# Softmax attention in a tuned encoder block: queries' preparation written behind the scores, and a bias made by two operations in place of three

## The chip, the cores and the metric

The kernel runs on one core of a Trainium2 chip. A core has five engines that work side by side and wait for each other by semaphores: TensorE (PE, matrix products and transposes), VectorE (DVE), ScalarE (ACT), GpSimd (POOL) and SyncE (SP, which here only issues transfers). Each engine works through its own instructions strictly in order. PE writes its results into PSUM, from which DVE and ACT read them. The metric is device time in microseconds (us), as a median over runs.

## The reference, cut to what matters

One encoder layer on x of 1024 tokens by 1024 features, in float32: gated linear attention (GLA) beside windowed attention (SWA), both projected, gated and merged, then a SwiGLU feed-forward part. The change lies in SWA alone: 8 query heads, 2 key/value heads, head width 128, tokens in 8 blocks of 128, each block of queries looking at up to three blocks of keys.

```python
q = _rope(_rms_norm(q, q_g), pos); k = _rope(_rms_norm(k, k_g), pos)
scores = jnp.einsum("bnqhgd,bnkhd->bnhgqk", qb, kc) * (hd ** -0.5)
scores = jnp.where(mask, scores, -jnp.inf)
m = jnp.maximum(scores.max(axis=-1, keepdims=True), sink)
p = jnp.exp(scores - m)
denom = p.sum(axis=-1, keepdims=True) + jnp.exp(sink - m)
o = jnp.einsum("bnhgqk,bnkhd->bnqhgd", p / denom, vc)
```

## The kernel before

**Products.** Each float32 operand of a large product is split into a high part (ACT, a copy that rounds) and a low part (DVE, the difference), and a product is made of three matmuls: high by high, high by low, low by high. So each weight tile costs ACT one operation (`wh`, L70) and DVE one (`wl`, L72).

**The attention stage** works on 16 items: 2 groups of four query heads (g) by 8 blocks of queries (n). An item goes through these steps, one per slot of the loop:

- `a_load` fetches the raw queries `qr` by a transfer that SP issues.
- `a_prep`: the mean of squares (ACT `sq` L866, DVE `ss` L867), its inverse root `rs` (ACT `rl` L98 and L99, DVE L101 to L104), and the rotary positions (DVE L912, L914, L916, L917, which write `qn`). PE does nothing here.
- `a_turn`: PE turns the four heads over (L923), ACT takes the high part `sqh` from PSUM (L926), DVE the low part `sql` (L927). `k_turn` does the same for a block of keys (PE L900, ACT `kTh` L902, DVE `kTl` L903), and `k_prep` splits the values (ACT `vSh` L894, DVE `vSl` L895), in the first half alone.
- `a_scores`, once per head: three matmuls (L76, names `kTh,sqh`, `kTl,sqh`, `kTh,sql`), then DVE adds the band's mask, writes `p` and takes the row maximum `mx` (L941). After the fourth head DVE works out the bias `nm` (L948 to L950) and `es` (L952), ACT makes the four exponentials with bias `nm` and scale `rs` (L956, with row sums `dn`), DVE the inverse of the sum (`dn` L958, `rd` L960), POOL multiplies (`p` L962). The normalised scale of the queries, `rs`, is thus applied to the scores, not to the queries.
- `a_probs`, once per block of keys: PE turns `p` over (L973), ACT and DVE split it (`ph` L976, `pl` L977).
- `a_out`: up to nine matmuls (L76, names `ph,vSh`, `pl,vSh`, `ph,vSl`), ACT copies the result out (`sob` L987), SP stores it.

In a slot, different steps of different items stand behind each other. A tuple `order` sets in which order the steps of one slot are written down. Behind each step, `slot` spends its share of a number n of dense matmuls (L76, names `mm`, from projections that have nothing to do with attention): 26 per slot in the first two slots, then 15, so about one behind each of 14 steps. A step that gives PE nothing to do still takes its share.

**What sets the order on an engine.** On PE, the order of writing holds exactly (`manual_schedule`). On DVE, ACT, POOL and SP a scheduler orders instructions when the program is built; the order of writing is its priority, its own estimate of when an operand is ready decides the rest. The order is then fixed, and each engine waits at its next instruction.

**PSUM buffers.** All attention products and transposes take turns in four buffers (`ch`), the dense ones in four others (`mm`). A `ch` buffer comes free when ACT or DVE has read it last: `pl` for a transposed block of p, L941 for a head's scores, `sql` and `kTl` for turned queries and keys, `sob` for the output. Which buffer a new product gets is fixed at build time too.

Of the kernel before, what the change touches and what calls it, by code (L numbers as in the profile page):

```python
# [12 lines left out]
ALU = mybir.AluOpType  # L13
# [17 lines left out]
def body(tc, i, out):  # L31
    nc = tc.nc
    with ExitStack() as root:
# [8 lines left out]
        def nm(s):  # L42
            uid[0] += 1
            return f"{s}_{uid[0]}"
# [4 lines left out]
        def chtile(shape, dt=F32):  # L49
            return psc.tile(list(shape), dt, tag="ch", name=nm("ch"))  # L50
# [27 lines left out]
        def mm3(o, ah, al, bh, bl, start, stop):  # L78
            mm(o, ah, bh, start, False)
            mm(o, ah, bl, False, False)  # L80
            mm(o, al, bh, False, stop)
# [798 lines left out]
        def k_load(t):  # L880
            raws[t] = sw.tile([P, 256], F32, tag="kvr", name=nm("kvr"))
            need(("skv", t))
            nc.sync.dma_start(out=raws[t], in_=scr["skv", t][:, 256:512])
            keys[t] = sw.tile([P, 2, P], F32, tag="key", name=nm("key"))
            nc.sync.dma_start(out=keys[t].rearrange("p a b -> p (a b)"), in_=scr["key", t])
# [45 lines left out]
        def a_scores(g, n, h):  # L931
            a = att[g, n]
            if h == 0:
                a.p = sw.tile([P, 4, 384], F32, tag="p", name=nm("p"))
                a.mx = sw.tile([P, 4], F32, tag="mx", name=nm("mx"))
            w, p, mx = a.w, a.p, a.mx
            ks = slice(a.b0 * P, (a.b1 + 1) * P)
            mo = (a.b0 - (n - 1)) * P
            s = chtile((P, 384))
            mm3(s[:, :w], a.qh[:, h], a.ql[:, h], kTh[:, g, ks], kTl[:, g, ks], True, True)  # L940
            nc.vector.tensor_tensor_reduce(out=p[:, h, :w], in0=s[:, :w], in1=band[:, mo:mo + w],  # L941
                                           op0=ALU.add, op1=ALU.max, scale=1.0, scalar=-1e30,
                                           accum_out=mx[:, h:h + 1])
            if h < 3:
                return
            sk = sink[:, 4 * g:4 * g + 4]
            nm_ = sw.tile([P, 4], F32, tag="nm", name=nm("nm"))
            nc.vector.tensor_tensor(mx, mx, a.rs, op=ALU.mult)  # L948
            nc.vector.tensor_tensor(mx, mx, sk, op=ALU.max)
            nc.vector.tensor_scalar(nm_, mx, -1.0, None, op0=ALU.mult)  # L950
            es = sw.tile([P, 4], F32, tag="es", name=nm("es"))
            nc.vector.tensor_tensor(es, sk, mx, op=ALU.subtract)  # L952
            nc.scalar.activation(es, es, AF.Exp)
            dn = sw.tile([P, 4], F32, tag="dn", name=nm("dn"))
            for h in range(4):
                nc.scalar.activation(p[:, h, :w], p[:, h, :w], AF.Exp, bias=nm_[:, h:h + 1],  # L956
                                     scale=a.rs[:, h:h + 1], accum_out=dn[:, h:h + 1])
            nc.vector.tensor_tensor(dn, dn, es, op=ALU.add)  # L958
            rd = sw.tile([P, 4], F32, tag="rd", name=nm("rd"))
            nc.vector.reciprocal(rd, dn)  # L960
            for h in range(4):
                nc.gpsimd.tensor_scalar(p[:, h, :w], p[:, h, :w], rd[:, h:h + 1], None, op0=ALU.mult)  # L962
# [50 lines left out]
        for n in range(2 * KT):  # L1013
            g, t = divmod(n, KT)
            todo[n + 5].append((a_out, g, t))
            todo[n + 5] += [(a_probs, g, t, kb) for kb in range(3)]
            todo[n + 3] += [(a_scores, g, t, h) for h in range(4)]
            todo[n + 2].append((a_turn, g, t))
            todo[n + 1].append((a_prep, g, t))
            if n < KT:  # L1020
                todo[n + 1].append((k_turn, n))
                todo[n].append((k_prep, n))
                if n:
                    todo[n - 1].append((k_load, n))
            todo[n].append((a_load, g, t))
        order = (a_probs, k_prep, a_prep, a_scores, a_turn, k_turn, a_out, k_load, a_load)
        k_load(0)
        with tc.manual_schedule(engines={mybir.EngineType.PE}):
            for t, v in enumerate(todo):
# [507 lines left out]
```

## Time and profile before

| What | us |
|---|---|
| Median of 3 runs | 1645.83 (1645.22 to 1646.64) |
| The profiled execution's own time | 1645.61 |
| Its span (first to last instruction) | 1643.8 |
| PE busy | 1626.0 (99%) |
| DVE busy | 1251.4 (76%) |
| ACT busy | 842.6 (51%) |
| POOL busy | 76.0 (5%) |

The profile is of one execution. Busy time is the time in which an engine had an instruction running. A wait stands at the instruction that had to wait, with what released it. In a row of the timeline the first number is the start in us from the span's start, the second the duration. DVE's and ACT's durations overlap the next instruction a little, so what a queue advances by is the distance between starts. The granted PE clock was 1.00 in every stage. The attention stage with its scores runs from about 575 to 740 us.

### The profile page before, as it was taken

What the parts mean: (1) busy time and instruction counts of PE and PEld (TensorE: products, weight loads), DVE (VectorE), ACT (ScalarE), POOL (GpSimd) and SP (SyncE); (2) the same over time, 40 slices, a digit from 0 to 9 for tenths busy, and PEclk for the clock granted to TensorE, in tenths of its full rate; (3) what the DMA queues carried; (4) which work ended last, traced back from release to release, by engine and by line L of the source; (5) the groups of instructions that cost most, each with busy time, mean ns of one, the idle gap of its engine ahead of it and who ended that gap; (6) DMA issues with size and microseconds to landing.
All of it is one profiled execution on the core that took longest, in us unless ns stands there. A gap on an engine that the chain in (4) does not pass through costs nothing.

```text
span 1643.8 us, 23281 instructions
## 1 busy us (share of the span) xinstructions
PE 1626.0 (99%) x7588; PEld 1346.0 (82%) x7588; DVE 1251.4 (76%) x2559; ACT 842.6 (51%) x1762; POOL 76.0 (5%) x68
## 2 busy tenths in 40 slices
PE   9999999999999989999999999999999999999999
PEld 7888888888888778888888888888888888888887
DVE  8866665589986598867885678887777778779655
ACT  8622224468998666665554557333333333354442
POOL 0000000000000034540000000000000000000000
PEclk9999999999999999999999999999999999999999
DMA  7554334475554633248765544443334443596433
GB/s 238 176 178 148 115 122 135 173 250 173 179 161 129 191 108 97 77 138 280 225 205 175 168 146 145 140 149 109 109 115 147 142 147 129 177 341 193 149 98 119
DMA packets 168010, 262.91 MB, mean 160 GB/s; under 512 B 19324, under 2 KB 52860, under 8 KB 167888
## 3 DMA queue, kind: packets, MB, share of 16 engines
q1 hardware_dynamic: 167888, 261.42, 49.8%
q8 instruction: 60, 0.98, 0.2%
q14 instruction: 62, 0.51, 0.1%
HBM read 187.93 MB, written 73.42 MB: 159 GB/s over the span
## 4 chain that ended last, share of the span: by engine, by line
PE 84%; DVE 9%; ACT 4%; DMA 2%; issue 1%; POOL 1%; SPq 0%; ACTq 0%; DVEq 0%
PE mm L76 23%; PE mm L306 9%; PE mm L308 9%; PE mm L307 9%; PE mm L1350 7%; PE ch L1350 5%; PE ch L76 4%; PE ch L306 4%; PE ch L308 4%; PE ch L307 4%; PE ch L460 3%; PE mm L460 2%; ACT p L956 1%; DVE wl L72 1%; DVE cs L655 1%
## 5 line engine op out<-in xcount | busy, mean ns | idle before, releaser
L298 ACT ACTIVATE wh<-ws 128x512 fp32r<-128x512 f32 x132 | 83.3, 632 | 195.9 <-PE mm L307 102.2
L70 ACT ACTIVATE wh<-wr 128x512 fp32r<-128x512 f32 x202 | 124.9, 626 | 87.4 <-PE mm L76 54.9
L72 DVE TENSOR_TENSOR wl<-wr,wh 128x512 fp32r<-128x512 f32 x202 | 137.7, 686 | 26.8 <-ACT wh L70 26.4
L299 DVE TENSOR_TENSOR wl<-ws,wh 128x512 fp32r<-128x512 f32 x132 | 90.5, 686 | 22.7 <-ACT wh L298 22.6
L298 ACT ACTIVATE wh<-wr 128x512 fp32r<-128x512 f32 x69 | 43.6, 632 | 124.8 <-issue 49.7
L962 POOL TENSOR_SCALAR p<-p,rd 128x384 f32<-128x384 f32 (+1 forms) x64 | 75.8, 1202 | 657.1 <-DMA qr<-sq 587.2
L298 ACT ACTIVATE wh<-a 128x512 fp32r<-128x512 f32 x64 | 40.5, 633 | 91.4 <-PE ch L1350 42.3
L76 PE MATMUL mm<-wh,xl 128*128 128x512 f32 x192 | 83.1, 433 | 0.0
L76 PE MATMUL mm<-wh,xh 128*128 128x512 f32 x192 | 79.6, 415 | 0.0
L76 PE MATMUL mm<-wl,xh 128*128 128x512 f32 x192 | 79.6, 414 | 0.0
L299 DVE TENSOR_TENSOR wl<-a,wh 128x512 fp32r<-128x512 f32 x64 | 44.2, 691 | 43.1 <-ACT wh L298 42.5
L1350 PE MATMUL mm<-hh,wh 128*128 128x512 f32 x176 | 68.5, 389 | 0.0
L1350 PE MATMUL mm<-hl,wh 128*128 128x512 f32 x176 | 68.5, 389 | 0.0
L1350 PE MATMUL mm<-hh,wl 128*128 128x512 f32 x176 | 68.5, 389 | 0.0
L76 PE MATMUL mm<-xl,wh 128*128 128x512 f32 x160 | 64.5, 403 | 0.1
L76 PE MATMUL mm<-xh,wh 128*128 128x512 f32 x160 | 64.4, 403 | 0.2 <-ACT wh L70 0.2
L76 PE MATMUL mm<-xh,wl 128*128 128x512 f32 x160 | 59.2, 409 | 0.0
L1320 DVE TENSOR_TENSOR hl<-hr,hh 128x512 fp32r<-128x512 f32 x75 | 51.4, 685 | 3.7 <-ACT hh L1319 3.7
L1350 PE MATMUL ch<-hh,wh 128*128 128x512 f32 x132 | 51.3, 389 | 0.0
L1350 PE MATMUL ch<-hl,wh 128*128 128x512 f32 x132 | 51.3, 389 | 0.0
L1350 PE MATMUL ch<-hh,wl 128*128 128x512 f32 x132 | 51.3, 389 | 0.0
L76 PE MATMUL mm<-oah,wh 128*128 128x512 f32 x128 | 50.2, 392 | 0.0
(620 smaller groups left out, 5077.7 us busy)
## 6 DMA issues: line engine op xcount, KB each, us to landing
wr<-in_w_fi_dram SPq DMA_DIRECT2D x102, 256.0 KB
wr<-in_w_f_dram SPq DMA_DIRECT2D x80, 256.0 KB
wr<-in_w_t_dram SPq DMA_DIRECT2D x56, 256.0 KB
B<-c SPq DMA_DIRECT2D x44, 256.0 KB
T<-tx SPq DMA_DIRECT2D x44, 256.0 KB
a<-in_w_fo_dram SPq DMA_DIRECT2D x44, 256.0 KB
hr<-T SPq DMA_DIRECT2D x44, 256.0 KB
wr<-in_w_ob_dram SPq DMA_DIRECT2D x32, 256.0 KB
```

The costliest lines, as they stand in the source:

```text
L70: nc.scalar.activation(h, raw, AF.Copy)
L72: nc.vector.tensor_tensor(l, raw, h.bitcast(F32), op=ALU.subtract)
L76: nc.tensor.matmul(o, a, b, start=start, stop=stop)
L298: nc.scalar.activation(h, src, AF.Copy)
L299: nc.vector.tensor_tensor(l, src, h.bitcast(F32), op=ALU.subtract)
L306: nc.tensor.matmul(o, h[:, c], x[kk][0], start=start and kk == 0, stop=False, skip_group_check=True)
L307: nc.tensor.matmul(o, h[:, c], x[kk][1], start=False, stop=False, skip_group_check=True)
L308: nc.tensor.matmul(o, l[:, c], x[kk][0], start=False, stop=kk == nk - 1, skip_group_check=True)
L460: nc.tensor.matmul(ys[m], a[:, c], b, start=f0, stop=f1, skip_group_check=True)
L962: nc.gpsimd.tensor_scalar(p[:, h, :w], p[:, h, :w], rd[:, h:h + 1], None, op0=ALU.mult)
L1320: nc.vector.tensor_tensor(l, r, h.bitcast(F32), op=ALU.subtract)
L1350: nc.tensor.matmul(ys[m], a[:, c], b, start=f0, stop=f1, skip_group_check=True)
```

## The change

Two edits. In `a_scores` the running maximum is multiplied by −1 and `rs` in one operation (`mx` = −mx·rs), and the bias is then the smaller of −sink and that (`nm` = min(−sink, mx)), where before it took a product, a maximum and a change of sign. `es` is now sink + nm, the same number as before. That is one DVE operation fewer per item, 16 in all. In `order`, `a_scores` moves from behind `k_prep` and `a_prep` to directly behind `a_probs`.

```diff
             nm_ = sw.tile([P, 4], F32, tag="nm", name=nm("nm"))
-            nc.vector.tensor_tensor(mx, mx, a.rs, op=ALU.mult)
-            nc.vector.tensor_tensor(mx, mx, sk, op=ALU.max)
-            nc.vector.tensor_scalar(nm_, mx, -1.0, None, op0=ALU.mult)
+            nc.vector.scalar_tensor_tensor(mx, mx, -1.0, a.rs, op0=ALU.mult, op1=ALU.mult)
+            nc.vector.scalar_tensor_tensor(nm_, sk, -1.0, mx, op0=ALU.mult, op1=ALU.min)
             es = sw.tile([P, 4], F32, tag="es", name=nm("es"))
-            nc.vector.tensor_tensor(es, sk, mx, op=ALU.subtract)
+            nc.vector.tensor_tensor(es, sk, nm_, op=ALU.add)
...
-        order = (a_probs, k_prep, a_prep, a_scores, a_turn, k_turn, a_out, k_load, a_load)
+        order = (a_probs, a_scores, k_prep, a_prep, a_turn, k_turn, a_out, k_load, a_load)
```

The lines behind L950 are one lower in the changed kernel. What the edits do to the engines' orders is seen at three places.

**PE, a slot in the middle of the stage**, from the last transposes of `p` to the second head's scores. Before:

```order
L973 MATMUL ch_7725<-ident,p_7467 128x128 x4
L76 MATMUL mm_7621<-xh_91,wh_7204 128x512
L76 MATMUL mm_7621<-xl_107,wh_7204 128x512
L76 MATMUL mm_7622<-xh_2805,wh_7204 128x512
L76 MATMUL ch_7757<-kTh,sqh_7673 128x384
L76 MATMUL ch_7757<-kTl,sqh_7673 128x384
L76 MATMUL ch_7757<-kTh,sql_7674 128x384
L76 MATMUL mm_7622<-xl_2806,wh_7204 128x512
L76 MATMUL ch_7763<-kTh,sqh_7673 128x384
```

Now:

```order
L972 MATMUL ch_7720<-ident,p_7442 128x128 x4
L76 MATMUL mm_7607<-xh_91,wh_7195 128x512
L76 MATMUL ch_7732<-kTh,sqh_7668 128x384
L76 MATMUL ch_7732<-kTl,sqh_7668 128x384
L76 MATMUL ch_7732<-kTh,sql_7669 128x384
L76 MATMUL mm_7607<-xl_107,wh_7195 128x512
L76 MATMUL mm_7608<-xh_2805,wh_7195 128x512
L76 MATMUL ch_7739<-kTh,sqh_7668 128x384
```

Two dense matmuls fewer stand ahead of the first scores, and here one fewer ahead of the second (in the slot before this one, two fewer). They stand behind the fourth scores now. The second scores wait for a `ch` buffer: before, in this slot, the one from which L941 reads the first scores; now, in every slot but a few, the one from which the first `pl` reads.

**ACT, the same slot**, from the turned queries' high part to the first high part of `p`. Before:

```order
L926 ACTIVATE sqh_7673<-ch_7668 128x512
L902 ACTIVATE kTh<-ch_7678 128x2x128
L987 COPY sob_7694<-ch_7684 128x512
L953 ACTIVATE es_7652<-es_7652 128x4
L956 ACTIVATE p_7606,dn_7655<-p_7606,nm_7648,rs_7310 128x384 x4
L976 ACTIVATE ph_7710<-ch_7705 128x512
```

Now:

```order
L926 ACTIVATE sqh_7668<-ch_7663 128x512
L902 ACTIVATE kTh<-ch_7673 128x2x128
L955 ACTIVATE p_7580,dn_7627<-p_7580,nm_7621,rs_7352 128x384
L952 ACTIVATE es_7624<-es_7624 128x4
L955 ACTIVATE p_7580,dn_7627<-p_7580,nm_7621,rs_7352 128x384 x3
L986 COPY sob_7689<-ch_7679 128x512
L975 ACTIVATE ph_7705<-ch_7700 128x512
```

The exponentials now stand ahead of the copy of the output, not behind it. On DVE, the three `pl` of a slot now stand ahead of all four L941; before, the first L941 stood ahead of them.

**DVE, the second slot that has scores**, from the turned queries' low part (`sql`); `kTl` is the low part of the keys that the next scores need. Before:

```order
L927 TENSOR_TENSOR sql_7150<-ch_7144,sqh_7149 128x512
L948 TENSOR_TENSOR mx_7098<-mx_7098,rs_6951 128x4
L903 TENSOR_TENSOR kTl<-ch_7154,kTh 128x2x128
L949 TENSOR_TENSOR mx_7098<-mx_7098,sink 128x4
L895 TENSOR_TENSOR vSl_6868<-kvr_7161,vSh_6860 128x256
L950 TENSOR_SCALAR nm_7123<-mx_7098 128x4
L952 TENSOR_TENSOR es_7127<-sink,mx_7098 128x4
L867 TENSOR_REDUCE ss_7174<-sq_7173 128x4
```

Now:

```order
L927 TENSOR_TENSOR sql_7149<-ch_7143,sqh_7148 128x512
L72 TENSOR_TENSOR wl_7197<-wr_7193,wh_7195 128x512
L895 TENSOR_TENSOR vSl_6868<-kvr_7160,vSh_6860 128x256
L867 TENSOR_REDUCE ss_7235<-sq_7234 128x4
L916 TENSOR_TENSOR qn_7247<-qr_7165,qA 128x512
L957 TENSOR_TENSOR dn_7106<-dn_7106,es_7103 128x4
L903 TENSOR_TENSOR kTl<-ch_7153,kTh 128x2x128
```

`kTl` now stands behind a split of weights, a part of the next query block's preparation, and the sum `dn`, which waits for the last exponential.

## The prediction

> **What bounds the kernel now.** I read the busy times by stage first. Columns: length, then busy time of PE, weight loads, DVE, ACT, POOL (instructions in brackets), PE clock, share of the DMA engines, GB/s.
>
> ```profile
> 575.00:600.00 25.00, 21.55 (x115) 17.58 (x114) 23.86 (x86) 16.18 (x47) 7.48 (x7) 1.00 0.38 113
> 600.00:650.00 50.00, 46.85 (x261) 39.34 (x260) 45.88 (x148) 34.66 (x93) 24.55 (x21) 1.00 0.30 93
> 650.00:740.00 90.00, 87.55 (x472) 73.30 (x471) 70.68 (x225) 59.88 (x153) 43.80 (x38) 1.00 0.35 111
> 740.00:1643.00 903.00, 900.09 (x3966) 744.00 (x3965) 688.11 (x1101) 388.61 (x654) 0.00 (x0) 1.00 0.51 164
> ```
>
> PE sets the time. The reader should look at what PE does not do: it idles 3.45, 3.15 and 2.45 us in the three parts of the attention stage, 9.05 together, and 2.91 us in the 903 us behind it. The change adds and removes no matmul, so it can only move these 9 us. The last row also gives the price of a dense matmul: 900.09 / 3966 = 0.23 us. What ended PE's waits in the stage (us in total, times, longest):
>
> ```profile
> PE ch L76 <- DVE mx L941: 2.6, 5, 0.5
> PE ch L923 <- DVE mx L941: 1.9, 1, 1.9
> PE ch L76 <- DVE pl L977: 1.8, 3, 1.0
> PE ch L973 <- POOL p L962: 0.9, 2, 0.6
> PE ch L76 <- DVE kTl L903: 0.6, 1, 0.6
> PE ch L923 <- DVE pl L977: 0.5, 1, 0.5
> PE ch L76 <- DVE rd L960: 0.4, 1, 0.4
> ```
>
> These are 8.7 us. Almost all are waits for a PSUM buffer that DVE has yet to read. The timeline splits them into a start-up, and a regular loss of about half a microsecond per slot. The start-up:
>
> ```profile
> 577.21 0.39 PE L76 MATMUL ch<-kTl,sqh 128*128 128x256 f32 x1 [0.63 <-DVE kTl L903]
> 588.60 0.66 PE L923 MATMUL ch<-ident,qn 128*128 128x128 f32 x4 [1.86 <-DVE mx L941]
> 591.55 0.33 PE L973 MATMUL ch<-ident,p 128*128 128x128 f32 x1 [0.35 <-POOL p L962]
> 596.98 0.63 PE L923 MATMUL ch<-ident,qn 128*128 128x128 f32 x4 [0.48 <-DVE pl L977]
> ```
>
> That is 3.3 us; the other 8.7 − 3.3 = 5.4 us are the regular loss of ten slots. A typical one, PE first, then ACT, then DVE:
>
> ```profile
> 618.74 0.60 PE L923 MATMUL ch<-ident,qn 128*128 128x128 f32 x4
> 626.58 0.44 PE L76 MATMUL ch<-kTh,sqh 128*128 128x384 f32 x1 [0.54 <-DVE mx L941]
> ```
> ```profile
> 619.37 0.60 ACT L926 ACTIVATE sqh<-ch 128x512 fp32r<-128x512 f32 x1 [1.70 <-PE ch L923]
> 622.15 0.59 ACT L987 COPY sob<-ch 128x512 f32<-128x512 f32 x1 [1.91 <-PE ch L76]
> 622.74 0.70 ACT L956 ACTIVATE p<-p,nm,rs 128x384 f32<-128x384 f32 x1
> 625.41 0.19 ACT L956 ACTIVATION_READ_ACCUMULATOR p<-p,nm,rs 128x1 f32 x1
> 625.50 1.54 ACT L976 ACTIVATE ph<-ch 128x512 fp32r<-128x512 f32 x3
> ```
> ```profile
> 620.04 0.68 DVE L927 TENSOR_TENSOR sql<-ch,sqh 128x512 fp32r<-128x512 f32 x1
> 620.64 0.15 DVE L948 TENSOR_TENSOR mx<-mx,rs 128x4 f32<-128x4 f32 x1
> 621.18 0.41 DVE L912 TENSOR_TENSOR sq<-qr,qB 128x256 f32<-128x256 f32 x1
> 621.52 0.16 DVE L950 TENSOR_SCALAR nm<-mx 128x4 f32<-128x4 f32 x1
> 621.59 0.15 DVE L952 TENSOR_TENSOR es<-sink,mx 128x4 f32<-128x4 f32 x1
> 621.66 0.15 DVE L102 TENSOR_TENSOR rt<-rt,rl 128x4 f32<-128x4 f32 x1
> 625.63 0.16 DVE L958 TENSOR_TENSOR dn<-dn,es 128x4 f32<-128x4 f32 x1 [0.20 <-ACT p L956]
> 625.96 0.56 DVE L941 CUSTOM_DVE_ANT_0 p<-ch,band 128x384 f32<-128x384 f32 x1 [0.16 <-PE ch L76]
> 626.53 1.85 DVE L977 TENSOR_TENSOR pl<-ch,ph 128x512 fp32r<-128x512 f32 x3
> ```
>
> The chain to see: `nm` starts at 621.52 and could release the exponentials at about 621.65, but ACT sits idle until PE's output product ends, copies `sob` at 622.15, and starts them at 622.74. They end at 625.4; only then come `ph`, and `pl` at 626.53. PE, wanting a buffer for the second head's scores since 626.04, waits.
>
> **The change part by part.** *Three operations to two.* 16 DVE instructions go, each worth the distance of starts in the rows above, 621.59 to 621.66: 0.07 us, 1.1 us in all. It is on PE's path only where DVE is the late one, so I count it inside the residual below. The multiplied-and-compared form is not in the trace at this line; the same kind with 128x4 operands (L103, L104) starts its follower 0.07 us later too, so its cost lies between 0.07 and the 0.16 a row lasts, and I take 0.07. [...]
>
> *Scores ahead of preparation, start-up.* PE reaches the first scores three dense matmuls earlier (it skips the shares of two empty steps), and `kTl` is not ready earlier, because nothing ahead of it on DVE has changed: the 0.63 becomes 0.63 + 3 × 0.23 = 1.3 us. In the next slot, DVE comes to its `kTl` later. From the end of the first `kTl`, at about 577.1, DVE's new order has ahead of it six 512-wide pieces of 0.60 (620.04 to 620.64 is that distance), eight 256-wide of 0.34 (621.18 to 621.52), one more reduction of 0.60, and about ten small of 0.07: 3.6 + 2.7 + 0.6 + 0.7 = 7.6, so `kTl` is done near 585.0. PE is there when it was there before, near 583.1 (its 0.7 us of added wait and its three matmuls fewer cancel): a wait of about 1.9 us. But the scores are then read sooner, and the 1.86 at 588.60, where the L941 stood behind preparation and evictions, goes. So do the 0.35 and the 0.48, since the exponentials and `pl` come sooner against PE. Start-up: 3.3 before, 1.3 + 1.9 = 3.2 now, a gain of 0.1. Bounds: minus 2 (the 1.86 only moves) to plus 2.
>
> *Scores ahead of preparation, each slot.* Measured from the turning of the queries (618.74): `sql` starts at +1.30, ends 0.60 later, the two small operations follow, `nm` is there at about +2.1. ACT now has the exponentials next: 2.67 (622.74 to 625.41) and 0.09, end at +4.9. Then `sob`, 0.5, whose product ended at +3.4, so no wait; `ph` at +5.4 to +5.9; the first `pl` to about +6.6. PE came to the second scores at 626.04, which is +7.30, and comes 0.23 to 0.46 earlier now: +6.84 to +7.07. ACT's chain leaves 0.3 to 0.5 us to spare: the regular wait goes. What is late next is DVE's queue: between `es` and `pl` it holds preparation and weights, and where a pair of `st` evictions falls into it, 1.2 us more.
>
> ```profile
> 600.00:620.00 20.00, 17.89 (x101) 14.98 (x100) 19.54 (x59) 13.98 (x39) 10.87 (x10) 1.00 0.39 122
> ```
> ```profile
> L125 DVE TENSOR_TENSOR st<-mm,rstd 128x512 f32<-128x512 f32 x12 | 8.1, 685 | 1.4 <-PE mm L76 1.3
> ```
>
> Twelve evictions in the stage are six pairs, four of them in the regular part. I take 0.5 us of wait that remains for each, between nothing and a full 1.2: 2.0 us (0 to 4.8). Regular part: 5.4 − 2.0 = 3.4.
>
> *What moves with it.* The loads of `qr` are issued later, since the buffer's last reader, the preparation, is later; on SP some weight loads now stand ahead of them. A `qr` is used a slot after its load, about 10 us, so I cost this at nothing; it would cost up to a slot's preparation if that cover went. The stores of `sob` come some 2.5 us later and nothing in the stage waits for them.
>
> Sum: 0.1 + 3.4 = 3.5 us. 1645.61 − 3.5 = 1642.1 for the profiled execution; the median of the runs stands 0.2 above it, and rounded I take **1642.2**. What a measurement of this kernel can tell from no change is about 0.2%, 3.3 us: the forecast lies on that edge.
>
> **The rivals.** *DVE is full* (no gain to speak of). From 600 to 620 DVE is busy 19.54 of 20 us, and a fuller order cannot make room. Then PE's waits up to 650 (3.45 + 3.15 = 6.6) only change place, and the gain is what little DVE does less there, 0.5 us, plus half of the 2.45 us that PE idles behind 650: about 1.7 us, 1643.9. For it: that row. Against: preparation is made a slot ahead, so it can be late without PE noticing. *All regular waits go*: no residual, 5.5 us, 1640.3. For it: from 650 on DVE is busy 70.68 of 90 us. Against: the `st` pairs. *PE outruns the chain* (the slower side). The dense matmuls that stood ahead of the first scores covered the chain to `pl`. If `nm` is more than 0.4 us later than I work out, behind `sql` or an eviction, the exponentials are no earlier than before, and each of the twelve items with three transposed blocks pays the 0.23 to 0.46 moved: 12 × 0.35 = 4.2 us on top, 1649.8. It decides where the first `pl` ends later than 6.84 us after the turn. For it: a margin of 0.3 us. Against: `sob` is out of the way. *The gain is lost behind the stage*: with PE earlier at 740, weights might be late.
>
> ```profile
> 740.00:760.00 20.00, 20.00 (x89) 16.53 (x89) 14.36 (x23) 10.23 (x18) 0.00 (x0) 1.00 0.86 276
> ```
>
> The DMA engines are busy 0.86 there, which speaks for it; PE has no wait at all in that stretch, which speaks against. The time would be 1645.6. That the scheduler ignores the new order is ruled out by the orders shown.
>
> **How the numbers follow.** The forecast, a gain of 2 to 5 us, 0.48, of which 0.27 above 3.3 us; all regular waits go, 0.20; DVE is full, 0.19; lost behind, 0.05; PE outruns the chain, 0.08. Faster by over 0.2%: 0.27 + 0.20 = 0.47. Slower: 0.08. Within: the rest, 0.45. The range takes the forecast, the fuller gain and the two cases of little gain, and leaves out the slower one and the far tail of the faster: 1639.7 to 1646.0.
>
> **What would show it.** Right: PE's waits for L941 and `pl` at the scores, ten in the regular part, are down to three or four; the exponentials start within 0.2 us of `nm`, with `sob` behind them; at the start-up a wait for `kTl` of 1 to 1.5 us and one near 2 stand in place of 0.63 and 1.86. DVE's small operations at these lines are 16 fewer. PE's idle time from 575 to 740 falls from 9.05 to about 5.5 and that behind 740 stays near 2.9. Wrong: PE waits for `pl` in most slots, or DVE has no idle time from 575 to 660 and PE as much as before, or the waits behind 740 grow.

## The result and the profile after

| | Median, us | Runs, us |
|---|---|---|
| before | 1645.63 | 1644.29 to 1646.64 (7) |
| changed | 1640.33 | 1639.54 to 1641.92 (7) |

The ratio is 0.9972, with a 95% interval from 0.9963 to 0.9981: faster by 5.3 us. The forecast had the direction, and its range, which reaches from 6 us faster to no change, holds the time; the sum had 3.5 us. Of all the runs below one was in a slow state, 2736.82 us at a mean granted clock of 0.556 (PE's order of the change, other engines' priority of before), and it is left out of every comparison. The profiled execution of the changed kernel took 1639.85 us, with a span of 1638.1 us, 5.7 less than before. PE's busy time in the page of the changed kernel:

```profile
PE 1624.9 (99%) x7588; PEld 1347.0 (82%) x7588; DVE 1250.5 (76%) x2543; ACT 841.8 (51%) x1762; POOL 75.2 (5%) x68
```

Of the 5.7 us, 1.1 are PE busy for a shorter time (1626.0 before) with the same 7588 instructions; the other 4.6 are PE idle for less. Both are in the attention stage: PE's first transpose of a key, ahead of it, starts 0.20 us sooner than before (566.66 against 566.86), its last output product, `ch<-ph,vSl`, 5.77 us sooner (734.76 against 740.53). Where the idle time is, the stages of the changed kernel show, in the columns of the prediction's first fence:

```profile
575.00:600.00 25.00, 22.10 (x121) 18.36 (x120) 24.58 (x86) 16.45 (x48) 8.95 (x8) 1.00 0.38 112
600.00:650.00 50.00, 49.12 (x272) 41.20 (x271) 48.41 (x157) 36.36 (x101) 25.29 (x20) 1.00 0.35 105
650.00:740.00 90.00, 89.25 (x481) 75.54 (x480) 70.14 (x205) 60.19 (x149) 40.74 (x36) 1.00 0.39 118
740.00:1637.00 897.00, 894.33 (x3941) 739.29 (x3939) 684.53 (x1096) 385.24 (x648) 0.00 (x0) 1.00 0.51 164
```

PE idles 2.90, 0.88 and 0.75 us in the three parts of the attention stage, 4.53 together (before 9.05), and 2.67 us behind it (before 2.91). Of the gain in idle time most is in the regular part (5.60 before, 1.63 now); the start-up gave 0.55. The waits of PE in the stage, grouped:

```profile
PE ch L76 <- ACT kTh L902: 1.8, 1, 1.8
PE ch L76 <- DVE kTl L903: 1.1, 2, 0.9
PE ch L76 <- ACT sob L986: 0.9, 2, 0.4
PE ch L76 <- DVE pl L976: 0.6, 3, 0.2
```

The waits for L941, six before with 4.5 us, are gone altogether. The timeline of PE's waits: three at the start-up, five in the regular part.

```profile
576.82 0.38 PE L76 MATMUL ch<-kTl,sqh 128*128 128x256 f32 x1 [0.90 <-DVE kTl L903]
584.28 0.44 PE L76 MATMUL ch<-kTh,sqh 128*128 128x384 f32 x1 [1.77 <-ACT kTh L902]
584.95 0.45 PE L76 MATMUL ch<-kTl,sqh 128*128 128x384 f32 x1 [0.23 <-DVE kTl L903]
602.33 0.44 PE L76 MATMUL ch<-kTh,sqh 128*128 128x384 f32 x1 [0.43 <-ACT sob L986]
603.55 0.44 PE L76 MATMUL ch<-kTh,sqh 128*128 128x384 f32 x1 [0.20 <-DVE pl L976]
643.12 0.38 PE L76 MATMUL ch<-kTh,sqh 128*128 128x256 f32 x1 [0.17 <-DVE pl L976]
677.46 0.44 PE L76 MATMUL ch<-kTh,sqh 128*128 128x384 f32 x1 [0.45 <-ACT sob L986]
678.68 0.44 PE L76 MATMUL ch<-kTh,sqh 128*128 128x384 f32 x1 [0.20 <-DVE pl L976]
```

And a regular slot of the changed kernel in the timelines of ACT and of DVE, beside the prediction's slot of before:

```profile
616.92 0.60 ACT L926 ACTIVATE sqh<-ch 128x512 fp32r<-128x512 f32 x1 [1.91 <-PE ch L923]
618.88 0.71 ACT L955 ACTIVATE p<-p,nm,rs 128x384 f32<-128x384 f32 x1 [1.09 <-DVE nm L949]
621.76 0.56 ACT L986 COPY sob<-ch 128x512 f32<-128x512 f32 x1
622.23 1.55 ACT L975 ACTIVATE ph<-ch 128x512 fp32r<-128x512 f32 x3
```
```profile
615.71 1.28 DVE L125 TENSOR_TENSOR st<-mm,rstd 128x512 f32<-128x512 f32 x2
618.63 0.15 DVE L949 SCALAR_TENSOR_TENSOR nm<-sink,mx 128x4 f32<-128x4 f32 x1
622.97 1.85 DVE L976 TENSOR_TENSOR pl<-ch,ph 128x512 fp32r<-128x512 f32 x3
```

`nm` starts at 618.63, the exponentials 0.25 later, and the copy `sob` comes behind them without a wait.

### The profile page after: what moved, and what is told of

The parts are those of the page before. It is cut to its first block, busy times and chain, and to the rows that moved or that the text cites. A ratio compares the mean times of both kernels' runs of the same rounds, so it can differ in the third digit from the quotient of the medians.

```text
span 1638.1 us, 23257 instructions
## 1 busy us (share of the span) xinstructions
PE 1624.9 (99%) x7588; PEld 1347.0 (82%) x7588; DVE 1250.5 (76%) x2543; ACT 841.8 (51%) x1762; POOL 75.2 (5%) x68
## 4 chain that ended last, share of the span: by engine, by line
PE 85%; DVE 10%; ACT 3%; issue 1%; DMA 1%; SPq 0%; ACTq 0%; DVEq 0%
PE mm L76 23%; PE mm L306 9%; PE mm L308 9%; PE mm L307 9%; PE mm L1349 7%; PE ch L1349 5%; PE ch L76 4%; PE ch L306 4%; PE ch L308 4%; PE ch L307 4%; PE ch L460 3%; PE mm L460 2%; DVE wl L72 1%; DVE cs L655 1%; PE ch L972 1%
```

## The experiments

Three theories stand behind the expectations. **A**, from the prediction: what counts is whether the exponentials stand ahead of the output's copy on ACT; a slot in which the copy stands first costs about 0.54 us. **B**: the gain is DVE's, by one operation fewer per item. **C**: the dense matmuls moved behind the fourth scores make it. A quantity for A can be read off for any kernel: a copy that stands first mostly makes ACT wait for PE's product. For before, after and the two edits apart, the row on `sob` says how long ACT waited ahead of copies in the stage (us, times); in this order:

```profile
  PE ch L76: 16.9, 10
```
```profile
  PE ch L76: 0.2, 1
```
```profile
  PE ch L76: 7.3, 5
```
```profile
  PE ch L76: 4.0, 3
```

The one wait of the change, 0.17 us at 735.2, is at the last copy of the stage, which no exponentials follow: in the change no copy stands first. The table sets that count beside PE's idle time, each worked out from the same stretches as above (length less PE's busy time). "Start-up" is 575 to 600 us, "regular" 600 to 740.

| Kernel | Median, us (runs) | Ratio, 95% | Copies waited | Idle, start-up | Idle, regular |
|---|---|---|---|---|---|
| before | 1645.63 (7) | | 10 | 3.45 | 5.60 |
| the order alone | 1642.40 (11) | 0.9974 to 0.9992 | 5 | 1.43 | 3.54 |
| the bias alone | 1641.45 (9) | 0.9968 to 0.9987 | 3 | 2.76 | 2.30 |
| both (the change) | 1640.33 (7) | 0.9963 to 0.9981 | 1 | 2.90 | 1.63 |
| PE's order of the change, other engines' priority of before | 1641.9 (10) | 0.9969 to 0.9988 | 1 | 3.88 | 2.48 |
| the change, but PE's order of before | 1637.17 (5) | 0.9938 to 0.9963 | 2 | 0.84 | 1.25 |
| the same with three operations | 1641.95 (11) | 0.9970 to 0.9988 | 8 | 0.84 | 4.35 |
| the change with one more DVE operation | 1641.81 (11) | 0.9968 to 0.9986 | 0 | 3.14 | 1.58 |
| the change with one more exponential | 1648.09 (11) | 1.0008 to 1.0026 | 2 | 3.50 | 6.03 |
| preparation behind the turning | 1638.81 (5) | 0.9952 to 0.9979 | 0 | 0.13 | 2.82 |

The kernel before, run on the same chips, took 1645.0 to 1645.3.

**The order alone.** Only the tuple; three operations stay.

```diff
-        order = (a_probs, k_prep, a_prep, a_scores, a_turn, k_turn, a_out, k_load, a_load)
+        order = (a_probs, a_scores, k_prep, a_prep, a_turn, k_turn, a_out, k_load, a_load)
```

> The scores are written ahead of the preparation, but the bias is still made by three operations. Theory A (what counts is whether the exponentials stand ahead of the output's copy on ACT; a slot where the copy is first costs PE 5.4 / 10 = 0.54 us): of 13 slots with three or two blocks in the stage's regular part the copy is first in 10 before, in 5 here, so the gain is 5 x 0.54 = 2.7 us, 1642.9. Theory B (what counts is the DVE operation saved): no gain, 1645.6. Theory C (what counts is that PE's dense matmuls moved from ahead of the first scores to behind the last): the whole gain of the change, 1640.3.

Measured 1642.40, close to A's number, but in part by luck. Half of the copies still stand first, and 3.54 us of regular idle time stay: five copies fewer gave 2.06 us, 0.41 each. Another 2.02 us of idle time went at the start-up, for which A had no term, and the medians, 2.8 us apart on the same chip, do not show all of it.

**The bias alone.** Only the operations; PE's order is that of before, instruction for instruction.

```diff
-            nc.vector.tensor_tensor(mx, mx, a.rs, op=ALU.mult)
-            nc.vector.tensor_tensor(mx, mx, sk, op=ALU.max)
-            nc.vector.tensor_scalar(nm_, mx, -1.0, None, op0=ALU.mult)
+            nc.vector.scalar_tensor_tensor(mx, mx, -1.0, a.rs, op0=ALU.mult, op1=ALU.mult)
+            nc.vector.scalar_tensor_tensor(nm_, sk, -1.0, mx, op0=ALU.mult, op1=ALU.min)
...
-            nc.vector.tensor_tensor(es, sk, mx, op=ALU.subtract)
+            nc.vector.tensor_tensor(es, sk, nm_, op=ALU.add)
```

> The bias is made by two operations, the order of writing is that of before. PE's order is that of before, word for word. Theory A: the copy is first in 3 of 13 slots, the gain is 7 x 0.54 = 3.8 us, 1641.8. Theory B: the whole gain, 1640.3. Theory C: none, 1645.6.

Measured 1641.45, again as A had it: 3.7 us below the kernel before on the same chip, from an edit that saves 16 operations of 0.07 us, 1.1 us at most. Regular idle time is 3.30 us less, 0.47 for each of seven copies. C falls as the cause of the regular gain, since no matmul moved. The place is to be seen on ACT, in the slot that the prediction showed of before:

```profile
622.07 0.71 ACT L955 ACTIVATE p<-p,nm,rs 128x384 f32<-128x384 f32 x1 [1.21 <-DVE rt L101]
...
624.95 0.56 ACT L986 COPY sob<-ch 128x512 f32<-128x512 f32 x1
625.42 1.55 ACT L975 ACTIVATE ph<-ch 128x512 fp32r<-128x512 f32 x3
```

The copy, which started at 622.15 before, stands behind the exponentials now. ACT's order is fixed when the program is built; that the shorter chain to `nm` is what made the scheduler place the exponentials sooner is an inference, the new place is not. The start-up keeps its longest wait, 1.89 us in place of the 1.86.

**One more DVE operation, one more exponential.** Both stand on the changed kernel. The first makes `es` by way of a copy of `nm`; PE's order stays that of the change, and on ACT only small operations (`es` and `rl`) change places. The second adds an exponential ahead of the four, into a tile that nobody reads.

```diff
-            nc.vector.tensor_tensor(es, sk, nm_, op=ALU.add)
+            nc.vector.tensor_scalar(es, nm_, 1.0, None, op0=ALU.mult)
+            nc.vector.tensor_tensor(es, sk, es, op=ALU.add)
```

> The changed kernel with one small DVE operation more per item (es by way of a copy of nm), so as many as before; the orders of ACT and PE are those of the changed kernel. Theory A: at most the 16 operations' own 16 x 0.07 = 1.1 us where DVE is late, 1640.3 to 1641.4. Theory B (DVE is full, and the operation saved is the gain): back to 1645.

```diff
+            xx = sw.tile([P, 384], F32, tag="xx", name=nm("xx"), bufs=1)
+            nc.scalar.activation(xx[:, :w], p[:, 0, :w], AF.Exp, bias=nm_[:, 0:1], scale=a.rs[:, 0:1])
```

> The changed kernel with one exponential more per item (the first head's, into a tile that nobody reads), ahead of the others on ACT; the exponentials still stand ahead of the output's copy. It delays ACT's chain to the first pl by 0.6 us per slot. Theory A (that chain ends PE's waits, with 0.3 to 0.5 us to spare): 0.1 to 0.3 us of wait come back in each of 13 slots, 1.3 to 3.9 us, 1641.6 to 1644.2. If DVE's queue alone sets when pl comes: 1640.3.

With the DVE operation back in place, 1641.81, and PE's idle time is that of the change within 0.2 us (3.14 and 1.58 against 2.90 and 1.63). B falls. The 1.5 us between the medians are not in the waits; the last section has where they are.

The exponential costs much more than expected: 1648.09, slower than before, though only two copies wait. So A is right in its direction, but it isn't the position of the copy that costs, it is how late `ph` starts. The slot above shows why the price is so high. `pl` starts at 622.97, and its first of three ends near 623.6; PE's second scores, and the dense matmul ahead of them, start at

```profile
623.23 0.39 PE L76 MATMUL mm<-xh,wh 128*128 128x512 f32 x1
623.68 0.44 PE L76 MATMUL ch<-kTh,sqh 128*128 128x384 f32 x1
```

and the load of their weights has waited:

```profile
623.68 0.19 PEld L76 LDWEIGHTS ch<-kTh,sqh 128*128 128x128 f32 x1 [0.48 <-DVE pl L976]
```

By the prediction's price, 900.09 / 3966, PE starts 0.23 us behind a dense matmul, and here it starts 0.45 behind: it is held by `pl` for 0.22 us. The profile lists no wait of PE: the row in front lasts 0.39, to 623.62, and leaves 0.06 us of it uncovered. So in this slot there is no margin at all, where the prediction had 0.3 to 0.5.

An exponential advances ACT by 0.69 (620.38 to 621.07 in the slot of the change), so up to that much could come back in each of 13 slots, 9.0 us in all; the medians are 7.8 apart. Of these, 5.0 us are in the stage's idle time (9.53 against 4.53), 4.4 of them in the regular part, 0.34 a slot, and 1.7 are a spell of half clock (the last section). The rest isn't placed.

**PE's order apart from the other engines'.** The first kernel writes preparation ahead of the scores, as before, but lets PE spend the dense shares as in the change. The second does the reverse: preparation is written behind the fourth scores, while its dense shares stay ahead of the first. The core of the second:

```diff
+                prep = [e for e in v if e[0] in (k_prep, a_prep)]
...
+                        fs[last - 1] = lambda e=v[last - 1]: run([e] + prep)
+                        fs[k:k] = [lambda: None for _ in prep]
```

> As the changed kernel with PE's order of it, but the preparation is written ahead of the first scores. Theory A: the copy is first in 1 of 13 slots, the gain is 9 x 0.54 = 4.9 us, 1640.7. Theories B and C: the whole gain, 1640.3. If the priority of the scores on DVE counts by itself, less than that: 1643.

> As the changed kernel, but PE's order is that of before: the two shares of dense matmuls stay ahead of the first scores, while the preparation is written behind the fourth. Theory A: the copy is first in 2 of 13 slots, the gain is 8 x 0.54 = 4.3 us, 1641.3. Theory C: none, 1645.6. Theory B: the whole gain, 1640.3.

The first came 1.2 us later than A had it (1641.9), with the worst start-up of all: 1.22, 0.64, 0.57 and 1.44 us of waits. Its time lies between the 1640.3 of B and C and the 1643 expected if the scores' priority on the other engines counts by itself, so this priority has a part in it. The second took 1637.17, 3 us less than any theory had (4 less than A), and 3.2 below the change. In its start-up, the waits for `kTl` and `kTh` are gone. PE's order alone covers the first: `kTl` starts at 576.38 here and at 576.35 in the change, but PE has dense matmuls to do until then. The second is another matter, since PE reaches the second slot's first scores when it reached them in the change. ACT and DVE there, first of the change, then of this kernel:

```profile
583.28 0.59 ACT L955 ACTIVATE p<-p,nm,rs 128x256 f32<-128x256 f32 x1
583.87 0.36 ACT L902 ACTIVATE kTh<-ch 128x256 fp32r<-128x256 f32 x1
```
```profile
584.48 0.41 DVE L903 TENSOR_TENSOR kTl<-ch,kTh 128x256 fp32r<-128x256 f32 x1
```
```profile
580.77 0.38 ACT L902 ACTIVATE kTh<-ch 128x256 fp32r<-128x256 f32 x1
581.07 0.60 ACT L955 ACTIVATE p<-p,nm,rs 128x256 f32<-128x256 f32 x1
```
```profile
582.30 0.42 DVE L903 TENSOR_TENSOR kTl<-ch,kTh 128x256 fp32r<-128x256 f32 x1
```

Here `kTh` stands ahead of the four exponentials, in the change behind them; `kTl` follows it, 2.2 us sooner. So with the dense matmuls moved the change pays 2.90 us at the start-up: 0.90 by the cover lost, 2.00 by the order on ACT and DVE that was built with them; without, 0.84 stay, most of it two waits that the change does not have. The profiled executions are 3.5 us of span apart: 2.1 are these, 0.4 regular idle time, 0.9 PE's busy time (1624.9 against 1624.0). This kernel is the best of those that were run, together with one below.

**The same with three operations.** The bias of before in that kernel.

> PE's order of before, preparation written behind the scores, and the bias made by three operations as before. The output's copy stands ahead of the exponentials in 8 of 13 slots on ACT (2 with two operations). Theory A: 6 x 0.54 = 3.2 us more than with two operations, 1640.4. Theory that two operations count only by their 1.1 us of DVE time: 1638.3 at most.

Measured 1641.95: the third operation costs 4.8 us here, more than A's estimate. Eight copies stand first, and ACT waits 1.90 us ahead of one of them, as before the change:

```profile
619.33 0.59 ACT L987 COPY sob<-ch 128x512 f32<-128x512 f32 x1 [1.90 <-PE ch L76]
```

The start-up is the same 0.84 in both; the regular part differs by 3.1 us, half a microsecond for each of the six slots more that have the copy first. Another 1.7 are in PE's busy time, 1625.7 with three operations and 1624.0 with two; part of each wait stands there, as the slot of the change showed, but how much of the 1.7 that is was not measured.

**The start-up by itself.** If the start-up's waits are for keys, turning the keys a slot earlier should take them away. The edit was made on the change and on the best version, first for every block of keys, then from the second block on.

```diff
-                todo[n + 1].append((k_turn, n))
+                todo[n].append((k_turn, n))
```
```diff
-                todo[n + 1].append((k_turn, n))
+                todo[max(n, 1)].append((k_turn, n))
```

> The changed kernel with the turning of the keys (k_turn) one slot earlier, so that kTh and kTl are ready long before the scores. Theory A with the start-up worked out as kTl being late behind the preparation and the exponentials: the start-up's 0.9 + 1.8 + 0.2 = 2.9 us of waits shrink to 0.5, 1637.9. If DVE's work as such is what is late there, the waits only change place: 1640.3.

> The kernel with the changed order but PE's order of before (1637.2), with the turning of the keys one slot earlier as well. There the start-up has 0.6 us of waits left, so 1636.6 to 1637.2; if the start-up were still bound by kTl, 2 us less.

> The changed kernel with the turning of the keys one slot earlier, from the second block of keys on; the first stays where it was, so that the 6.1 us wait for its load, which the earlier form brought, cannot come. Start-up theory (kTh and kTl are late behind the exponentials and the preparation): the 2.9 us of waits between 575 and 600 go, and with them the half clock that follows the 1.8 us wait in some executions: 1640.3 - 2.9 = 1637.4, spread under 1.5 us. Rival (DVE's work is late as such): the waits come back behind 600, 1640.3.

> The kernel with the changed order but PE's order of before (1637.2), with the same earlier turning of the keys. Its start-up has 0.6 us of waits, none of them for kTl: 1636.6 to 1637.4.

For every block, both missed: 1644.70 (0.9987 to 1.0005) and 1644.47 (0.9984 to 1.0002), no change against before. On the change PE was busy 25.00 of 25.00 us from 575 to 600, so the waits did go, but the first block's keys have not landed when PE turns to them:

```profile
566.95 0.66 PE L900 MATMUL ch<-ident,key 128*128 128x128 f32 x2 [6.07 <-DVE qA L860]
```

PE's clock is 0.50 to 0.51 in each piece of 2 us from 566 to 572, and 1.00 after. The wait is put down to DVE's `qA`; on the best version the same wait, 6.17 us, is put down to the transfer of `key`. From the second block on, 1637.86 on the change (0.9942 to 0.9967), close to what was expected, and 1637.18 on the best version (0.9938 to 0.9963), no better than without. On the change only part of the mechanism is in the trace, which is of the slowest of its five runs (1639.03): the start-up's idle time falls from 2.90 to 2.08, with 0.81 and 1.11 us now waited for `sql`. The number came out, its reason by less than half.

**Preparation behind the turning.** An order that leaves the scores where the change put them, and puts preparation behind the turning of queries and keys.

```diff
-        order = (a_probs, a_scores, k_prep, a_prep, a_turn, k_turn, a_out, k_load, a_load)
+        order = (a_probs, a_scores, a_turn, k_turn, k_prep, a_prep, a_out, k_load, a_load)
```

> The changed kernel with the preparation written behind the turning of the queries and keys as well (probabilities, scores, turns, preparation, output). The copy is never ahead of the exponentials on ACT. Two dense matmuls that stood ahead of the turn stand behind it, so kTl is asked for later against its making: the start-up's 2.9 us shrink by 0.5 to 1.5 us, 1638.8 to 1639.8.

Measured 1638.81, at the edge of what was expected, but by luck: the start-up's waits, of which 0.5 to 1.5 us were to go, are all but gone (0.13 us of idle time in place of 2.90), and 2.82 us of regular idle time are there in place of 1.63, though no copy waited. So the regular idle time isn't a function of the copy alone: with the copy behind in all or all but two or three slots it lies between 1.3 and 2.8, and with the extra exponential it is 6.03.

## Why the prediction was right, and where it was off

*PE's idle time in the attention stage bounds the gain.* Right: 4.5 of 5.7 us of span. The 1.1 us by which PE is busy less had no term in the sum. They are in the stage too (5.77 us between the same products). A row of 0.39 in front of a wait hides 0.39 − 0.23 = 0.16 us of it; the lists have 14 waits before and 8 now, so an estimated 6 × 0.16 = 1.0 us of the busy time is wait as well, and the 0.54 that a slot seemed to lose was 0.70. That the 1.1 us are this is an estimate, not a measurement.

*The exponentials come ahead of the copy, and the regular wait goes.* Right in mechanism, wrong in what is left to spare (see the rivals). Exponentials 0.25 us behind `nm` (0.2 predicted), `sob` behind them, waits for L941 none. The edits apart bear it out: from ten copies that waited to five to three to one, regular idle time goes 5.60, 3.54, 2.30, 1.63.

*2.0 us remain, 0.5 for each of four pairs of `st`.* This term was mis-sized, and its place was wrong. 1.45 us of regular waits remain, five of them, and four stand in two slots. In the slot shown above the pair at 615.71 falls ahead of `nm`, and the profile lists no wait of PE. Around 602, where two of the waits are, DVE has no `st` at all; PE waits for the copy itself, whose buffer the first scores take, since the copy now stands behind the exponentials. That wait, 0.43 and 0.45 us, was not among the costs: I had written that nothing in the stage waits for `sob`'s later place, with its stores in mind.

*Start-up: 3.3 before, 3.2 now.* Nearly right in sum, partly by luck: 2.90 (3.45 before, counted as idle time). The predicted waits, 1.3 and 1.9, measured 0.90 and 2.00 (1.77 + 0.23). `kTl` was to be done near 585.0 and ends at 584.9. But the 1.77 was ended by `kTh` on ACT, which I had not followed: it stands behind four exponentials that now come sooner, and DVE's `kTl` ends only the last 0.23. The 1.86, the 0.35 and the 0.48 did go.

*Three operations to two: 1.1 us at most.* Wrong as a cost of the edit, right as a cost of DVE's time. One more DVE operation per item leaves the waits as they are, and the runs at a clock of 1.000 average 1640.17 with it and 1639.97 without, no more than the distance of starts gives (1.1 us). The two operations of the new form cost about what was taken for them: in the slot shown, what follows them starts 0.07 and 0.08 us later (618.16 to 618.23 and 618.63 to 618.71). Yet the edit alone is worth 3.7 us, and with preparation written behind the scores on PE's order of before 4.8. Of that 3.3 and 3.1 us are regular idle time, which goes with the copy's new place on ACT. I had given that effect wholly to the tuple.

*The rivals.* "DVE is full" falls: from 600 to 650 DVE is busier than before (48.41 against 45.88) while PE idles 0.88 instead of 3.15. "All regular waits go" came nearest in time, 1640.3, but 1.45 us of them are there. "PE outruns the chain" did come by its own test, and only its price did not. In the slot shown the turn starts at 616.28 and the first `pl` ends near 623.6, 7.3 us behind it, where 6.6 was forecast and 6.84 was the limit. The exponentials start at +2.60 in place of about +2.14, as `nm` is later by some 0.4, behind `kTl` and small operations of the preparation; the rest was lost between them and the end of `pl`. PE is then held by 0.22 us. Part of the spare time had never been there: I took PE to come at 626.04, the end of the row in front, but 0.23 us behind that row's start it is 625.88. That the loss stayed near 0.2 us in such slots was luck as much as sum; the kernel with one more exponential shows what a longer chain costs, 1648.09. "Lost behind the stage": 2.67 us of idle time there against 2.91, no.

## What to carry to other kernels

Where a scheduler fixes each engine's order when the program is built, price an edit by what it moves on every engine, not by the operations it saves: here 1 us of DVE time moved a copy on ACT in six or seven slots and was worth 4 to 5 us. When a step is written later, ask separately what moves on the engine whose order is written by hand; leaving the dense matmuls ahead of the first scores was worth 3.2 us on top of the change. A list of PE's waits can be empty where PE is held all the same: compare the starts of two matmuls with the distance at which they follow each other elsewhere (at 623.68 it was 0.45 us against 0.23). And a chain without margin has no room: one exponential of 0.69 us more per item cost 7.8 us.

## What the runs showed of the hardware

A wait of PE of about 2 us (1.77 to 2.26) was followed by a spell of half clock (0.50) in some executions and not in others. The change with one more exponential, in pieces of 2 us (the clock is the third number from the end):

```profile
584.00:586.00 2.00, 0.74 (x3) 0.49 (x4) 2.00 (x10) 2.00 (x8) 0.42 (x1) 1.00 0.63 200
586.00:588.00 2.00, 2.00 (x9) 1.76 (x8) 2.00 (x6) 0.65 (x2) 2.00 (x3) 0.65 0.47 109
588.00:590.00 2.00, 2.00 (x7) 1.91 (x6) 1.31 (x5) 0.42 (x1) 1.46 (x2) 0.50 0.79 296
590.00:592.00 2.00, 2.00 (x12) 1.71 (x12) 1.59 (x7) 0.00 (x0) 0.00 (x0) 0.99 0.15 55
```

PE had waited 2.26 us up to 584.96; from about 586.6 to 590 its clock is 0.50. That is 3.4 us at half speed, so an estimated 1.7 us lost. The bias alone and the change with one more DVE operation show the same behind waits of 1.89 and 1.77: the clock is 0.92, 0.50 and 0.73 in the pieces from 588 to 594 of the first, 0.83, 0.50 and 0.81 in those from 586 to 592 of the second, which is 1.7 us lost in each again; the profiled execution of the change, with a wait of 1.77 too, kept 1.00. The granted clock that each run lists tells the two apart: of the change's seven runs, three have a mean of 0.999 and took 1641.69 to 1641.92, four have 1.000 and took 1639.54 to 1640.33. With one more DVE operation, seven runs at 0.999 average 1642.33 and four at 1.000 average 1640.17, beside 1639.97 for the change at 1.000: that is the 1.5 us that its waits did not show. Of the 47 compared runs of the six kernels in whose profile PE's longest wait is 1.44 us or less, none lists less than 1.000; of the kernel with preparation behind the turning, whose longest is 1.49, two of five do, its fastest and its slowest; with the 6 us waits all 22 do. The length alone doesn't decide, though: before, with its 1.86, lists less in 8 of 73 runs.

In these kernels, then, a wait of 1.77 to 2.26 us at PE cost its own length and, in some executions, an estimated 1.7 us more. What sets off the spell and what ends it, no run shows.
